# Keeping the split halves of two output weights in DRAM for the second token half

## The chip, the cores and the metric

The kernel runs on one core of one Trainium2 chip. The metric is the device time of one execution in microseconds, from the first instruction of the program to the last, as the runtime reports it. The profiled execution has a time of its own, and its span (first to last traced instruction) is a little shorter than that time.

## The reference

One decoder layer over 1024 tokens of 1024 channels, all in float32:

```
x = x + 1/2 * SwiGLU_1(RMSNorm(x))
h = RMSNorm(x)
[c_q | k_a | v_a | k_idx | w_idx | q_b | k_b | v_b | g_a | g_b] = h @ W_in
y_a = sparse attention (indexer scores -> top 256 keys of each query)     # (1024, 512)
y_b = stick-breaking attention                                            # (1024, 512)
merged = sigmoid(g_a) * (y_a @ w_o_a) + sigmoid(g_b) * (y_b @ w_o_b)      # (1024, 1024)
x = x + merged @ w_out
x = x + 1/2 * SwiGLU_2(RMSNorm(x))
```

The part at issue is the two products `y_a @ w_o_a` (512 x 1024 weights) and `merged @ w_out` (1024 x 1024 weights). Both are computed for one half of the tokens (512 rows) at a time, so each weight is used twice.

## The kernel before

**Split operands.** [...] Each operand is split into a high part (the value rounded, written by ScalarE, line 299 or 1124) and a low part (the value minus the high part, by GpSimd, line 301 or 1126). `mm3` (lines 312 to 314) then multiplies high by high, high by low and low by high into one PSUM bank. A weight piece is 128 x 1024 float32, 512 KB: its load needs one raw tile, its parts need two operand tiles. Splitting one piece takes one ScalarE copy and one GpSimd subtraction, and this is done again each time the piece is used.

**The weights come in pieces.** `w_o_a` is read in four pieces of 256 output columns (`d` = 0, 2, 4, 6). `w_out` is read in eight pieces, `n` = 0, 1 (column halves) by `j` = 0, 2, 4, 6 (pairs of 128-row blocks).

**The order of the work around the change.**

1. The attention stage is written as generators. A planner (`Weave`) with its own costs resumes whichever is ready first, and so fixes the order of TensorE, VectorE, ScalarE and GpSimd by hand. The weights arrive through `Feed`, which keeps three pieces coming; `weights()` loads a piece through the SP queue into the ring `oraw` (2 tiles) and splits it into the ring `ow` (4 tiles, so two pieces). At its end `project("oa", ...)` multiplies token half 1 by `w_o_a` (tiles named `oa0` to `oa6`, PSUM `psoa`), and `merged` stores the gated result to `md` in DRAM. The last two entries of the feed are the first two pieces of `w_o_a` once more (`woa0`, `woa2`), for the other half.
2. The `M0` loop (lines 2247 to 2263) multiplies the other token half by `w_o_a` (tiles `woa0` to `woa6`, PSUM `psm`). VectorE multiplies by a gate and adds the other branch (lines 2261, 2262, operands loaded at lines 2254, 2255), and the sum is split into eight tiles `M0` (lines 386, 387).
3. `project(0, M0, x0, merged)` multiplies the `M0` half by `w_out` (tiles `wout000` to `wout016`, PSUM `psout`). At `n` = 1, `j` = 2 it calls `merged`, which loads the other half's rows back from `md` (`m10r` to `m16r`, through the same ring of raw tiles) and splits them into `M1`.
4. `project(1, M1, x1, between)` multiplies the `M1` half by `w_out` again (tiles `wout100` to `wout116`); for `n` = 1 it holds all four pieces and finishes one row block after the other. The tiles of the second feed-forward block (`b0r`, `b1r`, `by`, `pst`) begin beside it.

From step 2 on the order on each engine and on the SP queue is made by the framework's scheduler, which simulates a timeline. Its tiles come from two rotations. `raw` has four places, two in the `outer` pool and two in `ring2`. `op` has nine, four in `outer` (tag `w`) and five in `ring2` (tag `r`):

```
op = in_turn((wt, 4), (lambda name: pool.tile([P, 1024], F32R, tag="r", name=name, bufs=NR), NR))
raw = in_turn((rawt, 2), (lambda name: pool.tile([P, 1024], F32, tag="raw", name=name, bufs=2), 2))
```

A tile in a rotation is written only when the work on the one that had its place, transfers from it included, is over. Each queue (SP's for loads and most stores, GpSimd's for `put_low` stores) works in order: a transfer that waits for a place holds those behind it. Some pieces of `w_in` already take the way through DRAM: `split_of` names their parts, and `weights()` loads such a piece as two parts.

Of the kernel before, what the change touches and what calls it, by code (L numbers as in the profile page):

```python
# [10 lines left out]
F32 = mybir.dt.float32  # L11
F32R = mybir.dt.float32r
# [10 lines left out]
PE, DVE, ACT, POOL, SP = "PE", "DVE", "Activation", "Pool", "SP"  # L23

P = 128
# [3 lines left out]
ND = D // P  # L29
# [29 lines left out]
def f32(ap):  # L59
    return ap.bitcast(F32)  # L60
# [34 lines left out]
class Weave:  # L95
# [92 lines left out]
    def give(self, *tiles):  # L188
        for t in tiles:
            self.held[t.tensor.name] -= 1  # L190
# [19 lines left out]
    def spawn(self, gen, rank=1, own=None):  # L210
        s = Stream(gen, rank, own or self.own)
        self.streams.append(s)
        self.step(s)
        return s
# [33 lines left out]
def trunk(ctx, tc, x, positions, g_ffn1, w1_gate, w1_up, w1_down, g_mix, w_in, g_cq, w_uq_a, w_q_idx,  # L248
          g_q_a, g_k_a, w_uv_a, w_o_a, w_o_b, w_out, g_ffn2, w2_gate, w2_up, w2_down, inv_freq, out):
    nc = tc.nc  # L250
    cst = ctx.enter_context(tc.tile_pool(name="cst", bufs=1))
    small = ctx.enter_context(tc.tile_pool(name="small", bufs=4))
    dram = ctx.enter_context(tc.tile_pool(name="dram", bufs=1, space=DRAM))
# [50 lines left out]
    def kview(k, n):  # L304
        return lambda raw: (raw[:, 0:k * n].rearrange("p (k f) -> p k f", k=k), k * n)

    def wcols(w, c0, n, k0, k, nm, **kw):
        return split(w[0, k0 * P:(k0 + k) * P, c0:c0 + n].rearrange("(k p) f -> p k f", p=P), nm, kview(k, n), **kw)
# [513 lines left out]

    columns = {f"wg{g}": C_GA + g * P for g in (*range(ND, 2 * ND), *range(ND))}
    columns.update((f"wqk{base}{pr}", base + pr * P) for pr in range(4) for base in (C_QB, C_KB))
    split_of = {nm: [dram.tile([P, 1024], F32, name=f"{nm}{part}d") for part in "hl"] for nm in columns}
    rows_of = w_in[0].rearrange("(k p) f -> p k f", p=P)


    put_high, put_low = nc.scalar.dma_start, nc.gpsimd.dma_start
# [24 lines left out]
    NR, NC_ = 5, 12  # L854
    ctx1, ctxf = ExitStack(), ExitStack()
    fpsum = ctxf.enter_context(tc.tile_pool(name="psf", bufs=1, space=PSUM))
    with tc.tile_pool(name="ring1", bufs=1) as rpool, tc.tile_pool(name="s1", bufs=1) as spool, tc.tile_pool(name="ps1", bufs=1, space=PSUM) as psum:
        op, raw = ring(rpool)
        bank = banks(psum, fpsum)
        sums, pair = of(spool, "s", 5, 512), of(spool, "pair", 2, 512, F32R)  # L860
        with tc.tile_pool(name="t1", bufs=1, side="right") as tpool, tc.tile_pool(name="c1", bufs=1) as cpool:
# [43 lines left out]
            def rows(t):  # L905
                xs.append(fp(tt if t > 3 else ts)(f"x{t}"))
                nc.sync.dma_start(xs[t], x[0, t * P:(t + 1) * P, :])
# [6 lines left out]
            first = [[load(w, q, f"a{e}r0") for q in range(2)] for e, w in enumerate((w1_gate, w1_up))]  # L914
# [86 lines left out]
        def after(n, p):  # L1001
# [10 lines left out]
            if n == 3 and p in range(5, 9):  # L1012
# [6 lines left out]
                     wt=lambda name: rpool.tile([P, 1024], F32R, tag="r", name=name, bufs=NR)) for j in range(2)]  # L1019
# [44 lines left out]
    with fp as fpool, psm as psum, tc.manual_schedule(  # L1064
            engines={nc.tensor.engine, nc.vector.engine, nc.scalar.engine, nc.gpsimd.engine}):
        weave = Weave(nc)
        give, spawn, mark = weave.give, weave.spawn, weave.mark
# [1118 lines left out]
        def merged(ps, load, row, half, to):  # L2186
# [9 lines left out]
            put_low(to, o)  # L2196
            give(o, *held)

        def project(nm, rows, halves, outs):

            for d in range(0, ND, 2):
                W = feed()
                yield PE, W
                wh, wl = W.parts
                for half in halves:
                    for e in range(2):
                        high, low = rows(half)
                        yield PE, high[0] if nm == "ob" else None, fbank
                        ps, r = fbank("ps" + nm), slice((d + e) * P, (d + e + 1) * P)
                        cols = slice(half * 512, half * 512 + 512)  # L2210
                        row, to = (ND + d + e, obd[r, cols]) if nm == "ob" else (d + e, md[r, :])
                        coming = spawn(gate_load(row, d + e, half, nm == "oa"))
                        for k in range(4):
                            yield PE, f"ya0{k}" if nm == "oa" else high[k]
                            c = slice((2 * k + e) * P, (2 * k + e + 1) * P)
                            mm3(ps, wh[:, c], wl[:, c], high[k], low[k], k == 0, k == 3)
                        outs.append(spawn((merged if nm == "oa" else gated)(ps, coming, row, half, to)))
                if nm == "ob":
                    for e in range(2):
                        mark(f"obd{d + e}", *outs[-4:])  # L2220
                give(*W.parts)
# [15 lines left out]
        first = [feed().parts for n in range(2)]  # L2237
# [6 lines left out]
    with ctxf, tc.tile_pool(name="ring2", bufs=1) as rpool, tc.tile_pool(name="ps6", bufs=1, space=PSUM) as psum:  # L2244
        op, raw = ring(rpool)
        bank = banks(psum, fpsum)
        with tc.tile_pool(name="m0", bufs=1) as mpool:
            M0 = []
            for d in range(0, ND, 2):
                wh, wl = first.pop(0) if first else wcols(w_o_a, d * P, 2 * P, 0, 4, f"woa{d}")  # L2250
                for e in range(2):
                    r = slice((d + e) * P, (d + e + 1) * P)
                    g = ht("gate", F32)
                    nc.sync.dma_start(g[:, 0:512], gd[r, 512:1024])
                    nc.sync.dma_start(g[:, 512:1024], obd[r, 512:1024])
                    ps = bank("psm", "bcda"[(d + e) % 4])
                    for k in range(4):
                        c = slice((2 * k + e) * P, (2 * k + e + 1) * P)
                        mm3(ps, wh[:, c], wl[:, c], Y[1][k][:, HI], Y[1][k][:, LO], k == 0, k == 3)
                    m = g[:, 0:512]  # L2260
                    nc.vector.tensor_mul(m, m, ps)
                    nc.vector.tensor_add(m, m, g[:, 512:1024])
                    M0.append(halve(mpool.tile([P, 1024], F32R, tag="m", name=f"m0{d + e}", bufs=8), m, nc.vector))
            hstack.close()
            ctx2, ctx3 = ExitStack(), ExitStack()
            tpool = ctx2.enter_context(tc.tile_pool(name="t2", bufs=1, side="right"))
            tt, ts = of(tpool, "t", 24, dt=F32R), of(tpool, "ts", 4, dt=F32R)
            fp = lambda place: lambda name: f32(place(name))

            def there(t):  # L2270
                return (t + NT // 2) % NT

            def residual(half):
                xs = []
                for q in range(4):
                    xs.append(fp(tt if half else ts)(f"x2{half}{q}"))
                    t = 4 * half + q
                    nc.sync.dma_start(xs[q], xd[there(t) * P:(there(t) + 1) * P, :])
                return xs

            def project(half, M, xs, between=None):

                for n in range(2):
                    c = slice(n * 512, n * 512 + 512)
                    ps = [bank("psout", "abcd"[q]) for q in range(4)]

                    def part(q, j, W):
                        h, l = slice(q * P, (q + 1) * P), slice(512 + q * P, 512 + (q + 1) * P)
                        for k in (j, j + 1):
                            wh, wl = (w[:, (k - j) * 512:(k - j + 1) * 512] for w in W)  # L2290
                            mm3(ps[q], M[k][:, h], M[k][:, l], wh, wl, k == 0, k == ND - 1)

                    def end(q):
                        nc.vector.tensor_add(xs[q][:, c], xs[q][:, c], ps[q])
                        t = 4 * half + q
                        nc.sync.dma_start(x2d[t * P:(t + 1) * P, c], xs[q][:, c])

                    Ws = {}
                    for j in range(0, ND, 2):
                        Ws[j] = wcols(w_out, n * 512, 512, j, 2, f"wout{half}{n}{j}", rawt=raw, wt=op)  # L2300
                        if n and j == 2 and between and not half:
                            between()
                        if not n or not half:
                            for q in range(4):
                                part(q, j, Ws[j])
                    if not n:
                        for q in range(4):
                            end(q)
                        if between and half:
                            between()  # L2310
                    elif not half:
                        for q in range(4):
                            end(q)
                    else:
                        for q in range(4):
                            for j in range(0, ND, 2):
                                part(q, j, Ws[j])
                            end(q)

            x0 = residual(0)  # L2320
            M1 = []

            def merged():
                for d in range(0, ND, 2):
                    m = raw(f"m1{d}r")
                    nc.sync.dma_start(m.rearrange("p (k f) -> p k f", k=2),
                                      md[d * P:(d + 2) * P, :].rearrange("(k p) f -> p k f", p=P))
                    M1.extend(halve(tt(f"m1{d + q}"), m[:, c], nc.vector) for q, c in enumerate((HI, LO)))

            project(0, M0, x0, merged)  # L2330
# [76 lines left out]
```

## Time and profile before

| | |
|---|---|
| median of 3 runs | 2126.56 us (2125.76 to 2130.45) |
| profiled execution, its own time | 2126.26 us |
| its span | 2124.5 us |
| TensorE busy | 2100.6 us, 99% of the span |
| VectorE, ScalarE, GpSimd busy | 72%, 50%, 43% |
| moved by the DMA engines | 387.79 MB, mean 183 GB/s |
| project("oa"), `psoa` | about 1308 to 1359 us |
| `M0` loop, `psm` | 1361 to 1391 us |
| `w_out`, first half, `psout` | 1391 to 1436 us |
| `w_out`, second half, `psout` | 1436 to 1484 us |

The times of the stages are those of the first and the last matmul into the PSUM tile, in us from the start of the span. In lines of the profile, `out<-in` are the tiles written and read, a duration stands behind the start time, and brackets give the idle time of the engine just before the instruction and what ended it. PE is TensorE, DVE VectorE, ACT ScalarE, POOL GpSimd; SPq and POOLq are their DMA queues. A line of a table by windows has the busy time and the instruction count of PE, PEld (weight loads), DVE, ACT and POOL, then the granted TensorE clock, the mean busy share of the 16 DMA engines, and the GB/s they moved.

### The profile page before, as it was taken

The numbers are of one execution on the slowest core, as the hardware profiler recorded it, in microseconds if no ns is written. First come the engines' busy times: TensorE is split into PE (matmuls) and PEld (weight loads), VectorE is DVE, ScalarE is ACT, GpSimd is POOL, SyncE is SP. The second block draws the span as 40 slices with busy tenths as digits, with TensorE's granted clock in tenths as the row PEclk, the third lists the DMA queues.
The fourth block names the chain that finished last, engine by engine and source line by source line (L and its number), as shares of the span: only waits on it lengthen the run. The fifth ranks groups of instructions, "written<-read, shape, count | busy, mean of one in ns | idle before, by whom it ended". The sixth has DMA issues, their size and how long they took to land.

```text
span 2124.5 us, 29820 instructions
## 1 busy us (share of the span) xinstructions
PE 2100.6 (99%) x10196; PEld 1762.4 (83%) x10196; DVE 1521.6 (72%) x2477; ACT 1063.6 (50%) x1998; POOL 913.5 (43%) x717
## 2 busy tenths in 40 slices
PE   8999999999999999999999999999999999999999
PEld 7888888888889988888887888778888888888887
DVE  7866767678875599788886588754755556488675
ACT  6343343334455356888886577535432322324443
POOL 6654555522345234322123342255665545542233
PEclk9999999999999999999999999999999999999999
DMA  5577877497685253686647755574143333259655
GB/s 150 160 245 219 251 203 237 151 328 249 212 231 167 76 159 105 224 217 165 171 157 231 258 165 169 190 257 151 50 129 100 104 95 129 95 185 330 222 175 188
DMA packets 298104, 387.79 MB, mean 183 GB/s; under 512 B 40144, under 2 KB 186224, under 8 KB 297952
## 3 DMA queue, kind: packets, MB, share of 16 engines
q1 hardware_dynamic: 285088, 343.90, 52.2%
q0 software_dynamic: 12864, 41.99, 5.5%
q8 instruction: 80, 1.31, 0.3%
q14 instruction: 72, 0.59, 0.1%
HBM read 264.67 MB, written 121.15 MB: 182 GB/s over the span
## 4 chain that ended last, share of the span: by engine, by line
PE 88%; issue 4%; DVE 3%; DMA 3%; POOL 1%; ACT 1%; SPq 0%; POOLq 0%; DVEq 0%; ACTq 0%
PE p L774 6%; PE p L775 6%; PE p L773 6%; PE pd L535 4%; PE pd L534 3%; PE pd L536 3%; PE pc L534 3%; PE pa L535 3%; PE pa L534 3%; PE pa L536 3%; PE pc L535 3%; PE pc L536 3%; PE psf L312 3%; PE psf L313 3%; PE psf L314 3%
## 5 line engine op out<-in xcount | busy, mean ns | idle before, releaser
L1374 ACT ACTIVATE junka<-u,cand,sig 128x1024 bf16<-128x1024 f32 (+3 forms) x124 | 134.5, 1085 | 5.0 <-DVE cand L1366 3.6
L1820 DVE TENSOR_TENSOR_SCAN left<-left,hidden 128x640 f32<-128x640 f32 (+3 forms) x64 | 88.9, 1409 | 2.0 <-ACT left L1814 1.8
L897 ACT ACTIVATE swh<-swr 128x512 fp32r<-128x512 f32 x48 | 30.2, 629 | 115.5 <-issue 52.5
L898 DVE TENSOR_TENSOR swr<-swr,swh 128x512 f32<-128x512 f32 x48 | 43.6, 908 | 37.8 <-ACT swh L897 37.6
L677 ACT ACTIVATE b0u<-b0u 128x512 f32<-128x512 f32 x20 | 12.6, 632 | 99.8 <-DVE b0u L557 84.4
L1874 DVE SCALAR_TENSOR_TENSOR pt<-pstT,pt 128x512 fp32r<-128x512 f32 (+1 forms) x96 | 51.4, 547 | 14.4 <-ACT pt L1871 13.8
L1871 ACT ACTIVATE pt<-pstT 128x512 fp32r<-128x512 f32 (+1 forms) x96 | 46.6, 495 | 16.6 <-PE pstT L1946 15.1
L1726 ACT ACTIVATE relu<-psdot 128x512 f32<-128x512 f32 (+1 forms) x80 | 40.7, 522 | 26.5 <-DVE u L1733 17.4
L1235 POOL DMA_DIRECT2D gd<-evg x32 | 18.0, 564 | 80.4 <-ACT evg L1230 59.4
L774 PE MATMUL p<-aT,aS 128*128 128x512 f32 x132 | 51.5, 390 | 1.0 <-DVE aT L387 1.0
L774 PE MATMUL p<-bT,bS 128*128 128x512 f32 x132 | 51.3, 389 | 0.0
L1733 DVE SCALAR_TENSOR_TENSOR u<-relu,WI,u 128x512 f32<-128x512 f32 (+1 forms) x70 | 49.2, 718 | 2.7 <-ACT relu L1726 1.7
L775 PE MATMUL p<-aT,aS 128*128 128x512 f32 x132 | 50.7, 389 | 0.0
L775 PE MATMUL p<-bT,bS 128*128 128x512 f32 x132 | 50.7, 389 | 0.0
L2000 ACT ACTIVATE e<-e,mx 128x768 f32<-128x768 f32 (+7 forms) x54 | 40.9, 759 | 13.3 <-DVE mx L1991 13.1
L773 PE MATMUL p<-bT,bS 128*128 128x512 f32 x132 | 47.0, 389 | 0.0
L1946 PE MATMUL pstT<-ident,left 128*128 128x128 f32 x288 | 45.8, 272 | 0.0
L773 PE MATMUL p<-aT,aS 128*128 128x512 f32 x132 | 44.9, 389 | 0.0
L1814 ACT ACTIVATE left<-psz 128x512 f32<-128x512 f32 (+2 forms) x96 | 43.4, 507 | 1.7 <-PE psz L1839 1.6
L1946 PEld LDWEIGHTS pstT<-ident,left 128*128 128x128 f32 x288 | 35.7, 140 | 8.2
L1370 DVE TENSOR_SCALAR_CACHE_REDUCE junkv<-u,cand 128x512 uint8<-128x512 f32 (+1 forms) x62 | 41.7, 673 | 0.8
L386 ACT ACTIVATE bT<-bt 128x512 fp32r<-128x512 f32 x44 | 26.2, 624 | 30.9 <-PE p L775 26.7
(3065 smaller groups left out, 8135.4 us busy)
## 6 DMA issues: line engine op xcount, KB each, us to landing
aw<-in_w_down_dram SPq DMA_DIRECT2D x33, 512.0 KB, 4.9
bw<-in_w_down_dram SPq DMA_DIRECT2D x33, 512.0 KB, 5.0
swr<-in_w_in_dram SPq DMA_DIRECT2D x48, 256.0 KB, 5.6
a0r<-in_w_gate_dram SPq DMA_DIRECT2D x22, 512.0 KB, 7.5
a1r<-in_w_up_dram SPq DMA_DIRECT2D x22, 512.0 KB, 7.2
b0r<-in_w_gate_dram SPq DMA_DIRECT2D x22, 512.0 KB, 4.1
b1r<-in_w_up_dram SPq DMA_DIRECT2D x22, 512.0 KB, 3.9
x<-in_x_dram SPq DMA_DIRECT2D x16, 512.0 KB, 6.2
```

The costliest lines, as they stand in the source:

```text
L312: nc.tensor.matmul(ps, ah, bh, start=first, stop=False)
L313: nc.tensor.matmul(ps, ah, bl, start=False, stop=False)
L314: nc.tensor.matmul(ps, al, bh, start=False, stop=last)
L534: nc.tensor.matmul(ps, a[:, c], b[k][:, HI], start=start and k == 0, stop=False, skip_group_check=True)
L535: nc.tensor.matmul(ps, a[:, c], b[k][:, LO], start=False, stop=False, skip_group_check=True)
L536: ins = nc.tensor.matmul(ps, a[:, l], b[k][:, HI], start=False, stop=k == 3, skip_group_check=True)
L773: nc.tensor.matmul(ps[q][m], S[:, h], T[:, HI], start=p == 0, stop=False)
L774: nc.tensor.matmul(ps[q][m], S[:, h], T[:, LO], start=False, stop=False)
L775: nc.tensor.matmul(ps[q][m], S[:, l], T[:, HI], start=False, stop=p == last)
L1374: nc.scalar.activation(junks[1][:, 0:(i + 1) * P], score[i], AF.Sign, scale=sig[:, b:b + 1], bias=cand.bitcast(F32)[:, b:b + 1], accum_out ...
L1820: nc.vector.tensor_tensor_scan(back, back, ones, 1.0, op0=ALU.mult, op1=ALU.max)
L1946: nc.tensor.transpose(tp[:, q * P:(q + 1) * P], A[n + q][:, j * P:(j + 1) * P], ident)
```

## The change

At its first use each piece's high and low part is also stored to DRAM through GpSimd's queue, and for the other token half the two parts are loaded through SP's queue in place of the raw piece; ScalarE's copy and GpSimd's subtraction of that second use are gone. For `w_o_a`, the new generator `weights_out` stores the parts of `oa0` to `oa6`; since `woa0` to `woa6` are now keys of `split_of`, `weights()` loads `woa0` and `woa2` as parts into `ow`, and the `M0` loop loads `woa4` and `woa6` as parts into `ring2` (tag `r`), where they were split in `outer` before. For `w_out`, `project(0, ...)` stores the parts of its eight pieces and `project(1, ...)` loads them into the `op` rotation, with no raw tile.

```diff
-    split_of = {nm: [dram.tile([P, 1024], F32, name=f"{nm}{part}d") for part in "hl"] for nm in columns}
+    split_of = {nm: [dram.tile([P, 1024], F32, name=f"{nm}{part}d") for part in "hl"]
+                for nm in (*columns, *(f"woa{d}" for d in range(0, ND, 2)), *(f"wout{n}{j}" for n in range(2) for j in range(0, ND, 2)))}
...
+        def weights_out(nm, *parts):
+            for to, w in zip(split_of[nm], parts):
+                weave.held[w.tensor.name] += 1
+                yield POOL, w
+                put_low(to, f32(w))
+                give(w)
+
         def project(nm, rows, halves, outs):
...
                 wh, wl = W.parts
+                if nm == "oa":
+                    spawn(weights_out(f"woa{d}", *W.parts))
...
-                wh, wl = first.pop(0) if first else wcols(w_o_a, d * P, 2 * P, 0, 4, f"woa{d}")
+                if first:
+                    wh, wl = first.pop(0)
+                else:
+                    wh, wl = (rpool.tile([P, 1024], F32R, tag="r", name=f"woa{d}{part}", bufs=NR) for part in "hl")
+                    for w, part in zip((wh, wl), split_of[f"woa{d}"]):
+                        nc.sync.dma_start(f32(w), part)
...
-                        Ws[j] = wcols(w_out, n * 512, 512, j, 2, f"wout{half}{n}{j}", rawt=raw, wt=op)
+                        kept = split_of[f"wout{n}{j}"]
+                        if half:
+                            Ws[j] = [op(f"wout1{n}{j}{x}") for x in "hl"]
+                            for w, d in zip(Ws[j], kept):
+                                nc.sync.dma_start(f32(w), d)
+                        else:
+                            Ws[j] = wcols(w_out, n * 512, 512, j, 2, f"wout0{n}{j}", rawt=raw, wt=op)
+                            for w, d in zip(Ws[j], kept):
+                                nc.gpsimd.dma_start(d, f32(w))
```

## The prediction

> **What bounds the kernel.** I read the engine shares first, then TensorE's waits in the stages of the change, then the DMA load by 10 us windows.
>
> ```profile
> span 2124.5 us, 29820 instructions
> PE 2100.6 (99%) x10196; PEld 1762.4 (83%) x10196; DVE 1521.6 (72%) x2477; ACT 1063.6 (50%) x1998; POOL 913.5 (43%) x717
> ```
>
> TensorE is busy for all but 23.9 us of the span, and the change removes no matmul. It can win only where TensorE waits in these stages, and lose wherever it makes a new wait. TensorE's waits from 1300 to 1500 us:
>
> ```profile
> PE psL L2037 <- DVE mx L1991: 2.4, 2, 2.2
> PE psm L312 <- DVE yt L1893: 1.4, 1, 1.4
> PE psout L313 <- POOL wout000l L301: 1.3, 1, 1.3
> PE pspT L2125 <- DVE mx L1991: 0.2, 1, 0.2
> ```
>
> That is 5.3 us in all, 0.25% of the span. I take 0.2%, 4.25 us, as what a measurement can tell from no change, so even the whole of it is barely a gain that would be seen. The other side is the DMA load:
>
> ```profile
> 1370.00:1380.00 10.00, 10.00 (x39) 8.03 (x38) 3.26 (x5) 1.70 (x3) 1.18 (x1) 0.85 1.01 359
> 1390.00:1400.00 10.00, 8.72 (x38) 6.87 (x37) 9.96 (x8) 4.85 (x6) 9.07 (x4) 1.00 0.31 105
> 1410.00:1420.00 10.00, 10.00 (x46) 8.28 (x45) 5.00 (x9) 5.05 (x9) 0.00 (x0) 1.00 0.92 331
> 1420.00:1430.00 10.00, 10.00 (x46) 8.29 (x45) 2.38 (x4) 1.83 (x3) 4.80 (x2) 1.00 1.01 380
> 1380.00:1436.50 56.50, 55.16 (x242) 44.75 (x240) 32.40 (x37) 20.91 (x28) 30.35 (x13) 1.00 0.72 258
> ```
>
> The last two numbers of a row are the busy share of the DMA engines and their GB/s. The transfers are already full at 1370 to 1380 and 1410 to 1430 us, where 359 and 380 GB/s is what they carry. The room is in the 1390s, at 105 GB/s.
>
> **The change, part by part.** Twelve pieces are stored as 24 parts of 512 KB (0.524 MB): 12.6 MB written. Twelve raw loads become 24 part loads: 6.3 MB more read. Twelve ScalarE copies and twelve GpSimd subtractions go; 24 GpSimd issues come.
>
> ```profile
> 1399.04 2.84 POOL L301 TENSOR_TENSOR wout006l<-wout006r,wout006h 128x1024 fp32r<-128x1024 f32 x1
> L2196 POOL DMA_DIRECT2D md<-o x8: 542/564/697, 1317.5 to 1362.9; - x8
> qad<-qsa POOLq DMA_DIRECT2D x8, 512.0 KB, 3.1
> L312 PE MATMUL psout<-wout006h,m x8: 389/389/389, 1409.1 to 1413.9; 128*128 128x512 f32 x8
> 1393.42 2.85 POOL L301 TENSOR_TENSOR wout002l<-wout002r,wout002h 128x1024 fp32r<-128x1024 f32 x1
> L313 PE MATMUL psout<-wout002l,m x8: 389/389/389, 1399.1 to 1403.2; 128*128 128x512 f32 x8
> ```
>
> *Store issues on GpSimd's queue.* Each holds it some 0.56 us (the `md` store), so two add 1.1 us per piece, and behind them waits the next piece's subtraction. The worst place is the run of four at the start of `w_out`, one after another on GpSimd today: the fourth, `wout006l`, ends at 1401.9; six store issues ahead of it make that 1405.3, and TensorE starts the piece at 1409.1. Cost 0, covered by 3.8 us; at 0.70 us an issue, the longest of that row, still by 3.0. A 512 KB store lands 3.1 us after its issue (`qad`), and only then is its place free; a place is next written four pieces of TensorE's work later, some 20 us, so that is covered too.
>
> *First piece of `w_out`, a gain.* Today GpSimd splits `woa4` and `woa6`, then `wout000`, whose raw tile has to wait for `woa4`'s place. Both splits go, so `wout000` is loaded and split earlier, and the 1.3 us wait goes: -1.3 us. What is late next is `wout002l`, which was ready at 1396.3 and is used at 1399.1, so nothing follows. Bounds -1.3 and 0.
>
> *`woa0`, `woa2` as parts.* Their load can start only when TensorE has left the places of `oa4` and `oa6`; the raw tile was fetched ahead.
>
> ```profile
> L314 PE MATMUL psoa<-y,oa6l x8: 388/389/393, 1350.0 to 1358.8; 128*128 128x512 f32 x8
> woa2r<-in_w_o_a_dram SPq DMA_DIRECT2D x1, 512.0 KB, 3.3
> 1361.33 0.47 PE L312 MATMUL psm<-y,woa2h 128*128 128x512 f32 x1
> 1363.46 0.39 PE L314 MATMUL psm<-y,woa2l 128*128 128x512 f32 x1
> 1363.69 0.39 PE L312 MATMUL psm<-y,woa2h 128*128 128x512 f32 x1
> 1339.18 2.38 POOL L1126 TENSOR_TENSOR oa6l<-oa6r,oa6h 128x1024 fp32r<-128x1024 f32 x1 [5.83 <-ACT oa6h L1124]
> ```
>
> `oa6` is done at 1359.2. The first part lands 3.3 us later, at 1362.5, the second 1.4 us after it (0.524 MB at 380 GB/s). TensorE now uses them at 1361.3 and 1363.5, as filling between the last attention products. It works in order, so a late part holds the products behind it: 1.2 us if the order stays, nothing if other work goes first, 2.1 us if all nine early matmuls (0.23 us apart) move behind the stretch. I take +1.0. On SP's queue the waiting loads stand ahead of `woa4`, whose new place comes free later than these (below); no cost. The stores of `oa0` to `oa6` go out when GpSimd is idle (it waited 5.8 us before `oa6l`): 0. They may shift the planner's order: no row shows that; I bound it by the largest wait there, 2.2 us either way, and take 0.
>
> *`woa4`, `woa6` as parts.* 2.1 MB fall into the full window 1370 to 1380, in place of 1.05 MB that came earlier.
>
> ```profile
> 1367.94 0.37 SPq L297 DMA_DIRECT2D wout002r<-in_w_out_dram x1
> 1379.91 0.39 PE L312 MATMUL psm<-y,woa4h 128*128 128x512 f32 x1
> 1377.39 1.28 DVE L2261 TENSOR_TENSOR gate<-gate,psm 128x512 f32<-128x512 f32 x2 [6.74 <-PE psm L314]
> 1378.60 3.49 DVE L2262 TENSOR_TENSOR gate<-gate 128x512 f32<-128x512 f32 x2
> L2262 DVE TENSOR_TENSOR gate<-gate x8: 679/690/2887, 1378.6 to 1399.5; 128x512 f32<-128x512 f32 x8
> 1386.03 1.88 DVE L387 TENSOR_TENSOR m<-gate,m 128x512 fp32r<-128x512 f32 x3
> 1391.16 1.07 PE L312 MATMUL psout<-wout000h,m 128*128 128x512 f32 x4
> ```
>
> Their new places are free from about 1368 (when the first load into that pool, `wout002r`, was issued); they are needed 12 us later and take 5.8 us at 359 GB/s. If they go first, the gate loads come up to 5.8 us later; VectorE's first product at 1377.4 waits, and TensorE needs `M0`'s first two tiles, ready by 1387.9, at 1391.2 (3.3 us of room). Against it, the two subtractions that slow VectorE here (3.49 us for two adds whose median is 0.69 us) are gone: 2.1 us back. I take 0; bounds -2 and +2.5 (5.8 less 3.3).
>
> *`w_out`, the crowd of transfers.*
>
> ```profile
> 1405.74 0.42 SPq L2326 DMA_DIRECT2D m10r<-md  x1
> 1415.40 0.37 SPq L297 DMA_DIRECT2D wout014r<-in_w_out_dram x1
> 1420.76 2.41 POOL L301 TENSOR_TENSOR wout014l<-wout014r,wout014h 128x1024 fp32r<-128x1024 f32 x1 [11.84 <-ACT wout014h L299]
> L312 PE MATMUL psout<-wout014h,m x8: 389/389/389, 1425.4 to 1430.2; 128*128 128x512 f32 x8
> wout100r<-in_w_out_dram SPq DMA_DIRECT2D x1, 512.0 KB, 9.1
> 1436.54 0.50 PE L312 MATMUL psout<-wout100h,m 128*128 128x512 f32 x1
> 1417.03 1.41 SPq L2278 DMA_DIRECT2D x<-xd  x3
> 1454.60 0.69 DVE L2294 TENSOR_TENSOR x<-x,psout 128x512 f32<-128x512 f32 x1 [3.52 <-PE psout L314]
> ```
>
> From 1380 to 1436.5, where the second half starts, 14.6 MB are moved (258 GB/s times 56.5 us). After: plus 8.4 MB of stores, less the five raw loads of the second half that land by then (2.6), plus the parts of `wout100` and `wout102` (2.1) and 1.05 MB of gate loads that the `woa` parts push past 1380: 23.5 MB. At 380 GB/s the stretch carries 21.5 MB; 2.0 MB, 5.3 us, do not fit. At 358 GB/s (the last window row, 258 at a share of 0.72) it is 3.3 MB, 9 us. Part can be late at no cost: the stores of `wout014` and `wout016` (2.1 MB), the four residual loads from 1417 on, added in at 1454.6 (2.1), and `wout102`, a piece later (1.05): 5.2 MB. But the queues work in order. Two deadlines are near: `wout014l` ends at 1423.2 and is used at 1425.6, with 2.4 us of room, while two pieces' stores (2.1 MB, 5.5 us) come into the stretch from 1405.7 to 1415.4 in which its raw tile waits for the `md` rows to come and go. `wout100` had 9.1 us landings with one transfer and now has two. Bounds 0 (all that is late is what can be) and +9; I take +2.5, nearer the lower end, since the early stores fit into the empty 1390s. In the second half ScalarE and GpSimd lose eight pieces' work, but TensorE has no wait there to win back.
>
> [...]
>
> **Sum.** -1.3 + 1.0 + 0 + 2.5 = +2.2 us on the profiled execution's 2126.26 us (span and 1.8 us around it), which is 0.3 us under the median shown: 2128.5 us.
>
> **The rivals.**
>
> *Slower: the transfers become the bound.* The misfit shows in full as a wait of TensorE for `wout014` or `wout100`: 5.3 to 9 us, 7.2 in the middle, less 1.3: 2132.2 us. It decides from 1.3 + 4.25 = 5.6 us of misfit on. For it: the 380 GB/s row and the 9.1 us landing; against it: 5.2 MB that can wait, and the row with 105 GB/s.
>
> *Faster: the waits go.* With twelve subtractions less, the waits of 2.2, 1.4 and 1.3 us and the slow clock of 1370 to 1380 (0.85, some 1.5 us) vanish: -6.4 us, 2119.9 us; it needs two thirds of it to count. For the 2.2 us wait speaks this:
>
> ```profile
> 1339.20 2.90 DVE L2087 TENSOR_TENSOR y<-yt,y 128x512 fp32r<-128x512 f32 x1
> 1342.75 0.45 PE L2037 MATMUL psL<-kkh,qs 128*128 128x384 f32 x1 [2.21 <-DVE mx L1991]
> ```
>
> An add of 0.69 us takes 2.9 beside the subtraction of `oa6l` (1339.18 to 1341.56, its row stands above), and TensorE waits. But `oa6l` is a first use and stays; only its moment could shift. The 1.4 us hang on the end of attention, which the change leaves alone.
>
> *Nothing at all:* only the 1.3 us go, or not even these, since the transfers find their room: 2125 to 2126.3 us. It lies inside the band of no change.
>
> **How the numbers follow.** Small net change, within 4.25 us either way (the forecast, and nothing at all with it): 0.52, with a range of its own of 2123 to 2130.5. Transfers as the bound: 0.40. Waits gone: 0.08. The likeliest gives 2128.5 us. The range leaves out the far ends: down to 2122.5 (the `w_out` gain and the bound of the planner's shift), up to 2136 (the 9 us end and the +1.0).
>
> **What would show it.** Right: no `wout000l` wait; TensorE waiting in the first half of `w_out` or at its end, by some 1 to 3 us, for a transfer or for `wout014`; a DMA share near 1 from 1400 to 1440. Wrong: more than 5 us of waits for `wout014` or `wout100` (the crowd mis-sized), a wait of TensorE for `woa4` or for `M0` (the gate loads pushed back), or a changed sum of waits before 1360 us (the planner's order).

## The result: slower, by 11 to 17 us

The changed kernel takes 2144.65 us (median of 4, 2143.78 to 2145.33) beside 2127.17 us of the kernel before (2125.76 to 2130.45): a ratio of 1.0080 [1.0062, 1.0097]. Measured again beside later experiments it took 2141.10 us (2140.49 to 2141.46), 1.0054 [1.0039, 1.0069]. Forecast were 2128.5 us and at most 2136. (The interval in brackets is the 95% interval of the ratio of medians.) The profiled execution of the first measurement spans 18.7 us more than before; TensorE's busy time grows by 6.1 us of it, with the same matmuls:

```profile
span 2143.2 us, 29848 instructions
PE 2106.7 (98%) x10196; PEld 1766.1 (82%) x10196; DVE 1517.0 (71%) x2477; ACT 1051.3 (49%) x1986; POOL 893.9 (42%) x729
```

The rest is waiting. TensorE's waits in this execution between 1300 and 1500 us (total, times, longest):

```profile
PE psg L414 <- DMA bg<-in_g_ffn_dram: 5.9, 1, 5.9
PE psout L312 <- ACT wout014h L299: 4.6, 1, 4.6
PE psL L2038 <- DVE mx L1992: 2.4, 2, 2.2
PE psm L312 <- DVE yt L1894: 1.4, 1, 1.4
PE psout L312 <- DMA wout100h<-wout00hd: 0.8, 1, 0.8
PE psout L313 <- POOL wout014l L301: 0.6, 1, 0.6
PE psm L312 <- DMA woa2h<-woa2hd: 0.6, 1, 0.6
```

The 1.3 us for `wout000l` are gone. New are 5.2 us at `wout014` (the piece in the middle of the first token half's second column block), 6.7 us at the start of the second half (the 4 KB of FFN gains, `bg`, whose transpose stands ahead of `wout100`, then `wout100h`), and 0.6 us for `woa2h`. The same execution by windows (TensorE busy first; PEclk, DMA share and GB/s last):

```profile
1410.00:1420.00 10.00, 10.00 (x45) 8.26 (x45) 4.84 (x5) 1.15 (x2) 4.72 (x6) 1.00 1.00 366
1420.00:1430.00 10.00, 6.52 (x29) 5.07 (x27) 2.91 (x6) 2.05 (x4) 0.00 (x0) 1.00 1.04 411
1430.00:1440.00 10.00, 8.29 (x23) 6.07 (x24) 3.32 (x4) 3.29 (x5) 6.84 (x6) 0.66 1.00 341
1440.00:1450.00 10.00, 6.02 (x27) 4.66 (x25) 3.78 (x7) 3.94 (x7) 0.57 (x1) 0.92 1.04 381
1450.00:1460.00 10.00, 7.25 (x26) 6.21 (x27) 3.00 (x10) 0.32 (x2) 1.67 (x3) 0.56 1.06 387
1460.00:1470.00 10.00, 10.00 (x48) 8.28 (x47) 0.01 (x1) 0.73 (x2) 0.00 (x0) 1.00 0.95 358
1380.00:1436.50 56.50, 51.31 (x217) 41.49 (x216) 36.13 (x36) 17.39 (x24) 25.11 (x22) 0.95 0.95 349
1380.00:1470.00 90.00, 78.07 (x326) 63.41 (x325) 42.91 (x54) 22.39 (x34) 29.93 (x28) 0.91 0.98 357
```

From 1410 us on the DMA engines are full, with a share of 0.95 to 1.06 in every 10 us. In the kernel before the long row reads

```profile
1380.00:1470.00 90.00, 88.62 (x404) 72.76 (x403) 50.60 (x64) 41.39 (x59) 47.37 (x23) 1.00 0.66 229
```

that is 20.6 MB in 90 us with a third of the time free, against 32.1 MB after. (The two rows cover the same clock time, not the same work: the changed kernel is behind by then.) Behind the two long waits TensorE's clock falls (0.66, then 0.92 and 0.56), and busy time times the missing share of the clock gives 2.8 + 0.5 + 3.2 = 6.5 us lost on top of 12.5 us of new waits.

**A cleaner measure than the span.** What lies ahead of the change scatters: the first product of the attention output (`psoa`, tile view) starts between 1308.1 and 1313.6 us in all profiles here, whatever was changed. So I also give the stage from there to the last product with `wout116h`: 1308.1 to 1483.8, 175.7 us before; 1310.7 to 1502.7, 192.0 us after. That is +16.3; in the second profile of the same kernel +14.4.

```profile
L312 PE MATMUL psoa<-y,oa0h x8: 389/391/474, 1310.7 to 1318.9; 128*128 128x512 f32 x8
```

```profile
L314 PE MATMUL psout<-wout116h,m x8: 389/389/389, 1490.7 to 1502.7; 128*128 128x512 f32 x8
```

(Tile views of the changed kernel; the numbers after the colon are the shortest, median and longest in ns, then the first and last start.)

### The profile page after: what moved, and what is told of

Its sections match the earlier page's. It is cut to its first block, busy times and chain, and to the rows that moved or that the text cites. A ratio compares the mean times of both kernels' runs of the same rounds, so it can differ in the third digit from the quotient of the medians.

```text
span 2143.2 us, 29848 instructions
## 1 busy us (share of the span) xinstructions
PE 2106.7 (98%) x10196; PEld 1766.1 (82%) x10196; DVE 1517.0 (71%) x2477; ACT 1051.3 (49%) x1986; POOL 893.9 (42%) x729
## 4 chain that ended last, share of the span: by engine, by line
PE 84%; DMA 5%; issue 4%; DVE 3%; ACT 1%; POOL 1%; SPq 0%; POOLq 0%; DVEq 0%; ACTq 0%
PE p L774 6%; PE p L775 6%; PE p L773 6%; PE pd L536 3%; PE pd L535 3%; PE pd L534 3%; PE pa L536 3%; PE pc L534 3%; PE pa L535 3%; PE pa L534 3%; PE pc L536 3%; PE pc L535 3%; PE psf L312 3%; PE psf L313 3%; PE psf L314 3%
## 5 line engine op out<-in xcount | busy, mean ns | idle before, releaser
L677 ACT ACTIVATE b0u<-b0u 128x512 f32<-128x512 f32 x20 | 12.6, 632 | 99.7 <-DVE b0u L557 84.4
L1872 ACT ACTIVATE pt<-pstT 128x512 fp32r<-128x512 f32 (+1 forms) x96 | 46.5, 494 | 16.6 <-PE pstT L1947 15.1
L1727 ACT ACTIVATE relu<-psdot 128x512 f32<-128x512 f32 (+1 forms) x80 | 40.7, 522 | 26.6 <-DVE u L1734 17.5
```

## The experiments

Four theories. **A**: the transfers are the bound, the `w_out` stores above all. **B**: order on SP's queue: the second half no longer uses raw places, so the second FFN's first loads go out ahead of `bg` and `wout100`. **C**: the `w_o_a` part pushes the gate loads, and all behind them, back. **D**: a part can be loaded only once its operand place is free, while a raw tile could be fetched ahead and split later.

| run | what | ratio to before | stage, us more than before |
|---|---|---|---|
| e1 | `w_o_a` part alone | 0.9988 [0.9978, 0.9997] | -2.0 |
| e11 | only `woa4`, `woa6` | 0.9996 [0.9987, 1.0005] | -1.9 |
| e12 | only `woa0`, `woa2` | 0.9992 [0.9983, 1.0001] | -1.1 |
| e2 | `w_out` part alone | 1.0079 [1.0064, 1.0094] | +18.4 |
| e4 | its stores alone | 1.0070 [1.0055, 1.0085] | +13.1 |
| e6 | stores of half the bytes | 1.0029 [1.0018, 1.0040] | +5.5 |
| e7 | stores of columns 0 to 511 | 1.0012 [1.0002, 1.0021] | +2.5 |
| e8 | stores of columns 512 to 1023 | 1.0036 [1.0024, 1.0048] | +6.2 |
| e5 | part loads alone | 1.0016 [1.0007, 1.0025] | +1.1 |
| e3 | change, gains in a place of their own | 1.0075 [1.0060, 1.0090] | +16.7 |
| e9 | change, FFN loads held | 1.0046 [1.0032, 1.0059] | +9.2 |
| e10 | change, TensorE kept busy | 1.0061 [1.0047, 1.0075] | +9.4 |
| e13 | e4, five stores held | 1.0047 [1.0032, 1.0062] | +11.3 |
| e14 | change, stores and FFN loads held | 1.0049 [1.0032, 1.0066] | +13.6 |
| e15 | change again | 1.0054 [1.0039, 1.0069] | +14.4 |

0.1% is 2.1 us. The two columns can differ by some microseconds for one run. The ratio is that of the medians, while the stage comes from one profiled execution, and that lies at the low end of its kernel's times for e1, e4, e5, e8 and e10 and at the high end for e2, e11, e12 and e14.

**Which half of the change: e1, e2.**

```diff
e1: - Ws[j] = [op(...) ...] and the stores     + Ws[j] = wcols(w_out, ...) in both halves
e2: - spawn(weights_out(f"woa{d}", ...)), part loads of woa   + wcols(w_o_a, ...)
```

> Only the w_o_a half of the change (its parts stored at first use, loaded as parts for the other token half); w_out is split twice as before. Theory A (the w_out stores are too much traffic between 1400 and 1460 us): no stores there, so at most 2 us over the kernel before, 2127 to 2130, and no wait for wout014h over 2 us. Theory B (queue order: FFN loads put ahead of the gains and of wout100 once the second half needs no raw places): the second half keeps its raw places here, so also 2127 to 2130. Theory C (the w_o_a part pushes the gate loads and with them the end of the first product, the releases and wout014 back by some 5 to 7 us): the wait for wout014h stays, 4 to 5 us and a slow clock behind it, 2132 to 2137.

> Only the w_out half of the change; w_o_a is loaded and split as before. Theory A: nearly the whole loss stays, 2139 to 2144, with waits for wout014 or the md rows of 4 us or more. Theory B: the wait for the gains (5.9 us in the changed kernel) and the slow clock behind it stay, and nothing ahead of them: 2133 to 2138. Theory C: wout014 comes in time, and what is left is 2 to 4 us under the changed kernel at least: 2132 to 2140, with the wait for wout014h under 2 us.

e1 is 2.6 us faster than the kernel before and has no wait of TensorE at all between 1380 and 1500 us, so theory C falls: its gate loads too are issued 2 to 3 us later than before (the first at 1370.9 us in place of 1368.9, the last at 1382.3 in place of 1379.5), and no wait follows. e2 has the whole loss. Its waits:

```profile
PE psg L414 <- DVE by L434: 4.6, 1, 4.6
PE psout L312 <- ACT wout014h L299: 3.7, 1, 3.7
PE psout L312 <- DMA wout100h<-wout00hd: 1.4, 1, 1.4
```

**The stores alone: e4.** (Half 1 splits `w_out` as before; what is stored is never read.)

```diff
+ if not half: nc.gpsimd.dma_start(d, f32(w))   # per part
  Ws[j] = wcols(w_out, ...)                     # both halves
```

> The kernel before with the 16 stores of w_out's parts added (8.4 MB out on the POOL queue) and nothing else: the second token half still loads and splits w_out itself, and what was stored is never read. Theory A: the stores alone make the crowd, 2135 to 2142, with waits of 3 us or more for wout014, wout016 or the md rows. Theory B: the second half keeps its raw places, so the FFN loads are not put ahead: 2127 to 2131. Theory C: w_o_a is as before, so 2127 to 2131.

14.9 us: the stores alone make most of the loss, as A says, though no FFN load is put ahead here and no part is waited for. The rows of `md` show how (landing time last), and the two largest rows of TensorE's waits:

```profile
m10r<-md SPq DMA_DIRECT2D x1, 512.0 KB, 14.1
...
m14r<-md SPq DMA_DIRECT2D x1, 512.0 KB, 17.3
```

```profile
PE pst L448 <- DVE by L434: 4.2, 2, 3.2
PE psout L312 <- ACT wout014h L299: 2.8, 1, 2.8
```

`m10r` landed in 7.5 us before. `wout014`'s raw tile takes the place of an `md` row that must land and be split first. The row is 6.6 us late, `wout014l` had 2.4 us of room, and TensorE waits 4.0 us for the piece, 2.8 for the high part and 1.2 more for the low. The larger row, for `by`, comes by another way. Two raw tiles of the second half land late (`wout102r` in 15.1 us, 9.7 before), so GpSimd's subtractions of `wout102` and `wout104` run from 1451.6 to 1456.4 us, beside VectorE's scaling of `by`: the first of a pair of these scalings takes 2.56 us there. In the kernel before a pair took 0.88 us with no subtraction of GpSimd beside it (two of the four), and 3.07 and 3.04 us beside one (`wout106l` and `wout112l`). No run tests this second way alone.

Stores issued after `m10r` seem to have slowed it as well: in e8 below one store was issued ahead of the row (at 1403.5 us, the row at 1404.9) and three behind it by 1410.3, and it still took 14.1 us. How the DMA engines divide their time between the two queues, no run shows.

In the whole change the late row is another one, and a second cause stands ahead of it. Counted from the first `psoa` product, `m12r` is issued 6.2 us later than before, and it lands in 12.9 us in place of 8.4, while `m10r` lands in 7.0. First the kernel before, then the changed one:

```profile
1403.12 0.69 DVE L387 TENSOR_TENSOR m<-gate,m 128x512 fp32r<-128x512 f32 x1 [0.70 <-ACT m L386]
1406.20 0.47 SPq L2326 DMA_DIRECT2D m12r<-md  x1
```

```profile
1403.85 7.07 DVE L387 TENSOR_TENSOR m<-gate,m 128x512 fp32r<-128x512 f32 x1 [0.70 <-ACT m L386]
1410.99 3.23 SPq L2293 DMA_DIRECT2D x<-xd  x4
1415.00 0.76 SPq L2349 DMA_DIRECT2D m12r<-md  x1
```

VectorE's last subtraction for `M0` takes 7.07 us in place of 0.69. It runs beside an unbroken run of subtractions and store issues on GpSimd, from 1397.2 to 1414.7 us. The four residual loads (`x<-xd`) stand on SP's queue until that subtraction is over, the queue's own waits say (7.9 us), and `m12r` stands behind them; ScalarE splits `m12r` and `m14r` ahead of `wout014h`. No run takes this cause away alone, and the runs that share it do not lose alike. e15 has it in full (7.08 us, landing 12.9) and waits 5.0 us for `wout014`. e14 below has 8.56 us there and issues `m12r` as late, but there the row lands in 7.7 us, and TensorE waits 1.1 us for the subtraction itself and only 0.5 us for `wout014`. So the late issue by itself brought little; with a slow landing it brought the 5 us.

**Bytes or issues, and which stores: e6, e7, e8.**

```diff
e6: - nc.gpsimd.dma_start(d, f32(w))   + nc.gpsimd.dma_start(d[:, HI], f32(w)[:, HI])
e7: - if not half:   + if not half and not n:          e8: + if not half and n:
```

> As the run with the stores alone, but each of the 16 stores writes only the left half of its part (128x512), 4.2 MB in place of 8.4; the same number of DMA issues in the same places. Theory A by bytes: 4.2 MB is under the 5 MB that could be put off, so most of the 15 us goes, 2128 to 2134. If the number of issues, their 0.55 us each on POOL's queue, or the operand places that the stores hold are the cause, little changes: 2138 to 2144.

> As the run with the stores alone, but only the 8 stores of the first four pieces (columns 0 to 511, 4.2 MB), which go out between 1393 and 1412 us. Theory A: they land on the rows of md asked for at 1404 to 1410 (14 us to land with all the stores, 7.5 us before), so the wait for wout014h stays at 1 to 3 us and the rest goes: 2129 to 2136.

> As the run with the stores alone, but only the 8 stores of the last four pieces (columns 512 to 1023, 4.2 MB), half of them between 1405 and 1413 us, half after 1430. Theory A: 2 MB less stand ahead of the rows of md than with all the stores, wout014 comes in time or less than 1 us late: 2127 to 2133, less than with the first four pieces.

Half the bytes with all 16 issues cost 6.2 us of 14.9 (2133.95 us, at the upper end of what the bytes had been given). Whatever the issues cost by themselves is within these 6.2 us, VectorE's long subtraction included (5.84 us here, 5.88 in e4), and the other half of the bytes makes 8.7 us, so the cost goes with the bytes in the main. The two halves alone cost 2.5 and 7.6 us; together 14.9, not 10.1: room used once is used. I had the order of the two wrong. The later stores cost more: they are issued from 1403.5 us on, just when the `md` rows are asked for, whose slowest landing is 15.1 us in e8 and 12.6 in e7; TensorE waits 3.5 us for `wout014` in e8 and 1.3 in e7, and only in e8 does the clock fall behind it (0.76). The 0.9 us for `wout010h` that e2, e4 and e6 show, and 1.0 in e7, are a place that a store held: in e4 the store landed at 1404.08 and ScalarE's copy began at 1404.12.

**The loads alone: e5.** (It loads kept parts of `w_in`'s gate columns in place of `w_out`'s.)

```diff
- kept = split_of[f"wout{n}{j}"]   + kept = split_of[f"wg{4 * n + j // 2}"]
- nc.gpsimd.dma_start(d, f32(w))
```

> The kernel before with the second half's loads of the change and without its stores: the second token half loads 16 parts of the same size and shape, but those kept of w_in's gate columns (stored long before) in place of w_out's, so its result is another; no w_out part is stored. Theory A (the bytes of the stores are the cause): 2126 to 2129, no wait over 1 us between 1400 and 1470 us. Theory D (a part can only be loaded once its operand place is free, which is when wout016 is used up, where a raw tile could be loaded ahead and split later): a wait of 4 to 7 us for wout100 and 2 to 4 us of slow clock behind it, 2132 to 2138.

```profile
PE psout L312 <- DMA wout100h<-wg0hd: 2.7, 1, 2.7
```

Theory D exists, but it is worth 1.1 us by the stage and 3.4 [1.5, 5.3] by the times, not 5 to 10; the clock stayed at 1.00 behind this wait.

**The gains in a place of their own: e3.**

```diff
- Right(g_ffn2, bank, fp(op), ...)   + Right(g_ffn2, bank, lambda name: cst.tile([P, P], F32, name=name), ...)
```

> The changed kernel with one thing altered: the FFN gains (4 KB) have a place of their own instead of one in the ring of operand places, so their load can go at the start and no load of wout100 stands behind it. Theory B: the 5.9 us wait and most of the slow clock behind it go, 2134 to 2138 (7 to 10 us less than the changed kernel). Theory A: the transfers are the bound, so the wait turns into one for wout100 or wout102 and 0 to 3 us are saved, 2141 to 2145. Theory C says of this wait what A says.

```profile
PE psout L312 <- issue: 7.6, 1, 7.6
PE psout L312 <- ACT wout014h L299: 5.4, 1, 5.4
```

("issue" is a wait for nothing that the profile records.) Nothing was won: `wout100h` now stood where `bg` had stood. SP's queue in the changed kernel and in e3 (start, us):

```profile
1433.97 5.21 SPq L2293 DMA_DIRECT2D x<-xd  x4
1439.28 0.71 SPq L500 DMA_DIRECT2D b0r<-in_w_gate_dram  x1
1440.10 6.72 SPq L410 DMA_DIRECT2D bg<-in_g_ffn_dram  x1
1446.99 0.34 SPq L2319 DMA_DIRECT2D wout100h<-wout00hd  x1
```

```profile
1437.78 0.65 SPq L500 DMA_DIRECT2D b0r<-in_w_gate_dram  x1
1438.61 6.88 SPq L2319 DMA_DIRECT2D wout100h<-wout00hd  x1
```

It is not the gains that are slow, but whatever follows the FFN loads on the queue.

**The FFN loads held, and TensorE kept busy: e9, e10.**

```diff
e9:  + if half and not n and j == 4: load the 4 tiles of w2_gate, w2_up here, in program order
e10: + if n and j == 4 and not half: 30 transposes of ident   # ahead of wout014
     - R.gain()   + R.gain(40)                                # 40 ahead of bg's
```

> The changed kernel with one order altered: the first four loads of the second FFN's weights (2.1 MB), which go out ahead of the gains and of wout100 at 1431 to 1449 us, are held until the second half's loads of wout100 to wout104 have been issued. Theory B (queue order): the gains and wout100h are issued at about 1440 in place of 1446.8, the wait of 5.9 us and the slow clock behind it go, 2134 to 2138. Theory A (bytes): the stores stand ahead of wout014 as before, so the wait of 4.6 us stays, and 0 to 4 us are saved, 2141 to 2145. Theory D (a part's load waits for its operand place): the gains are issued at 1440, but wout100 still waits for places and then 6 us for its landing: 2138 to 2142.

> The changed kernel with TensorE kept busy in its two long waits: 30 transposes of the identity (some 3.5 to 4 us) right ahead of wout014's first product, and 40 (some 5 us) ahead of the gains' transpose; their results are not used, and all transfers stay as they are. If the slow clock behind each wait is a loss of its own: PEclk stays at 1.00 between 1430 and 1460 us and 5 to 8 us are saved, 2136 to 2140. If what follows would have to wait for the transfers in any case: the clock is full, waits for wout016 or wout102 take the place, 2141 to 2145.

In e9 `bg` goes out in 0.55 us, and the wait at the start of the second half falls from 6.7 to 2.5 us; the one at `wout014` stays:

```profile
PE psout L312 <- ACT wout014h L299: 5.4, 1, 5.4
PE psout L313 <- DMA wout100l<-wout00ld: 2.2, 1, 2.2
...
PE psout L312 <- DMA wout102h<-wout02hd: 0.3, 1, 0.3
```

In e10 the clock is full behind the second wait (1.00 where it was 0.56):

```profile
1450.00:1460.00 10.00, 10.00 (x51) 8.47 (x50) 2.73 (x4) 5.02 (x8) 0.00 (x0) 1.00 1.06 391
```

Both medians came out where B and the clock theory put them (2136.75 and 2138.89 us), but not all of that is theirs. Both profiles also lack the 2.2 us wait for `mx` near 1345 us, ahead of every altered instruction. Less that, their stages are 3.0 and 2.8 us under the changed kernel's second profile. That is one pair of profiles each, and the times do not show it: 1.0046 and 1.0061 stand beside 1.0080 and 1.0054 for the changed kernel, and both intervals overlap that of the second, [1.0039, 1.0069]. In e10 the clock behind the first wait is still 0.85, and TensorE still waits 3.4 us at `wout014` and 1.8 at the start of the second half, so the run also shortened waits and does not weigh the clock alone.

**Bytes, or only their order: e13, e14, e15.**

```diff
+ if f"{n}{j}{x}" in ("06l", "10h", "10l", "12h", "12l"): held.append((d, w))
+ while n and j == 4 and held: store them, in program order   # behind wout014's split
```

> The run with the stores alone, same 16 stores and bytes, but five of them (wout006l, wout010h, 010l, 012h, 012l, 2.6 MB) are issued only after wout014's subtraction, behind wout014's own two stores. If the stores cost by sharing the engines with the md rows: these land in 8 to 10 us in place of 14, wout014 comes in time or under 1.5 us late, and over half of the 13 to 15 us goes, 2130 to 2135. If the bytes as such are too many between 1400 and 1460 us: the wait moves to wout016 or to the second half's pieces and under a third goes, 2138 to 2143.

> The whole change with both orders mended: the same five stores held until wout014 is split, and the second FFN's first four loads held until wout100 to wout104 have been issued. By sharing and order: no wait over 2 us at wout014 and at wout100, 2127 to 2133. By bytes: waits of 4 us or more at wout016, wout100 or wout102, 2134 to 2140.

> The changed kernel itself, beside the two above. If the slow clock near 1345 us (a 2.2 us wait for DVE's mx in the attention stage, then 3.7 us lost) differs from one execution to the next, its times spread by some 4 us and its profile may lack it: 2139 to 2146. If it belongs to the kernel: 2143 to 2146 with the wait there again.

e13 does what it should at the place: no wait for `wout014` is left, and `m10r` lands in 9.9 us. But much of the loss moves on (its largest rows in `w_out`; the one for `wout000l` is the old wait):

```profile
PE psout L312 <- ACT wout100h L299: 2.3, 1, 2.3
PE psout L313 <- POOL wout000l L301: 1.3, 1, 1.3
PE psout L313 <- POOL wout100l L301: 1.2, 1, 1.2
PE psout L312 <- ACT braw L469: 1.2, 1, 1.2
```

```profile
wout102r<-in_w_out_dram SPq DMA_DIRECT2D x1, 512.0 KB, 18.7
...
wout106r<-in_w_out_dram SPq DMA_DIRECT2D x1, 512.0 KB, 17.8
```

The second half's raw loads now take 18 us. It costs 10.0 us where e4 cost 14.9 (1.8 less by the stage), so a third of the loss goes, at the border of what the bytes had been given. e14, the whole change with both orders mended, is as slow as e15 beside it (1.0049 and 1.0054): `wout014` is down to 0.5 us, and the sum sits at the start of the second half:

```profile
PE psout L312 <- DMA wout100h<-wout00hd: 9.3, 1, 9.3
```

This alone does not make it the bytes, for a store that is held also holds the place of the part it stores, and the second half needs these places. In e14 `bg` was issued at 1439.4 us, just after a held store had landed (1439.25), and so were `wout100l`, `wout104h` and `wout104l`, each within 0.03 us of such a landing; the held stores took 10.5 to 15.9 us to land. In e13 ScalarE's copy into `wout100h` waited for a store that landed at 1442.3, though its raw tile was there at 1438.1. The engines were full at this point (share 1.03 to 1.12 from 1430 to 1470 us in e14), so these two runs leave open how much is the full engines and how much the places. That the bytes make the loss in the main rests on e4 beside e6. What e13 and e14 show is that to hold stores back wins a few microseconds at most.

e15 also tells the scatter. The wait for `mx` is there again, but with the clock at 1.00, where the first profile had 0.83 (first row the changed kernel, second row e15):

```profile
1340.00:1350.00 10.00, 7.79 (x29) 5.76 (x28) 9.73 (x21) 6.64 (x12) 2.95 (x2) 0.83 0.55 171
```

```profile
1340.00:1350.00 10.00, 7.81 (x45) 6.49 (x44) 9.83 (x20) 6.71 (x13) 3.69 (x5) 1.00 0.48 132
```

That is 1.3 us; with the 2.5 us by which e15's stage starts earlier it makes 3.8 of the 4.5 us between the two profiled spans of one kernel.

**The version to keep** is e1, the `w_o_a` part alone: 0.9988 [0.9978, 0.9997], 2.6 us under the kernel before, which is less than the 4.25 us that the prediction took as visible.

## Why the prediction was wrong

*Failed: the term "`w_out`, the crowd of transfers", +2.5 with bounds 0 and +9.* It measured +16.8 us (e2); apart, the stores cost 14.9 (e4) and the loads 3.4 (e5). The step that failed was the reckoning that all but 2 to 3 MB of the added transfers fit in or can wait at no cost. The mechanism was named rightly, and so were both deadlines that broke, `wout014` and `wout100`; what "would show it wrong" was more than 5 us there, and it was 11.9 with the wait for `bg`. Four things were wrong with the size:

- The window ended at 1436.5, where the second half begins, and 5.2 MB were called able to wait. What waits falls on the next 34 us, which the change fills as well, with 8.4 MB of parts in place of 4.2 MB of raw tiles and with FFN loads pulled forward. Over 1380 to 1470 us the row of before has a share of 0.66, so 31 us of room; the 11.5 MB more that were moved need 32 us at 357 GB/s. Put off in the sum, these bytes had no free room behind the window, only what the other transfers left.
- The stretch was taken to be full all along. The rate was not the fault: 380 GB/s came from the best 10 us, but once the engines were full, 60 us carried 364 to 374 GB/s in the changed kernel and 378 in e15. But over the 56.5 us the changed kernel carried 349, 19.7 MB of the 23.5 wanted, and the 3.8 MB left are 10.9 us. The early stores were to fill the empty 1390s, and they did not: 1390 to 1400 us carried 297 GB/s at a share of 0.77, and 204 at 0.59 in e15.
- "Able to wait" was read as "will wait". The packets of both queues took the time of the same 16 engines (in e4, from 1395 to 1450 us, 62.2% of it went to SP's queue and 37.7% to GpSimd's), and the `md` rows that `wout014` hangs on came later: `m10r` landed in 14.1 us for 7.5 in e4, and `m12r` in 12.9 for 8.4 in the changed kernel, where it was issued 6.2 us later besides.
- The slow clock behind a new wait was not counted: 6.5 us by the windows of the first profile. e10's profile gives some 3 us of it back; its times show nothing clear of noise.

The kernel's new waits and clock losses add up: 12.5 + 6.5, and 1.3 us of slow clock near 1345, less the 1.3 us for `wout000l` and the 1.5 us of slow clock near 1370 that the kernel before had, make 17.5 us; the stage is 16.3 longer.

*Only half right.* Store issues on GpSimd, 0: no piece of the first column block is late in the changed kernel, as reckoned. But the reckoning looked at GpSimd alone. VectorE's subtraction of 7.07 us beside that queue, and SP's queue behind it, were not in it. Nor does the cover for the places hold everywhere: without the `w_o_a` part TensorE waits 0.9 to 1.0 us for `wout010h`, whose place a store held (e2, e4, e6, e7).

*Right or nearly so.* First piece, -1.3: its wait is gone in e1, e11 and after. `woa4`, `woa6`, 0 (-2 to +2.5): e11 measured -0.9 [-2.8, +1.1], with the first piece's gain in it. `woa0`, `woa2`, +1.0 (0 to 2.1): e12 measured -1.7 [-3.6, +0.2], so the sign is not shown; the late part shows as predicted (0.3 to 0.6 us for `woa2h`), and whether more than that is won elsewhere was not traced. All of `w_o_a`: -0.3 forecast, -2.6 [-4.7, -0.6] measured. The gate loads did come later, by 2 to 3 us in e1 and so within the 3.3 us of room that the prediction gave them; no wait followed.

*The rivals.* "The transfers become the bound" is what happened, at 2132.2 us for 0.40; its price took over the same window and the same bytes that can wait, and so the same fault. "The waits go" did not come: in e1 only the 1.3 us wait went. "Nothing at all" is out by the measured interval.

## What to carry to other kernels

Before trading an engine's work for DMA bytes, add up the bytes over the whole stretch in which the transfers run full, to where they are idle again. Price them at the full rate, and count as room only the gaps that the order of the queues lets them use; a transfer "that can wait" is worth only the room behind it, and a store that waits keeps its place (here 0.9 to 1.0 us of waiting for `wout010h`). Where the added traffic shares the engines with a load that something hangs on, that load can slow at once (here `m10r`, landing in 14.1 us for 7.5 in e4), so late deadlines break before the total does. And a new wait on TensorE can cost more than its length: in the first profile here 6.5 us of slow clock stood behind 12.5 us of new waits.

## What the hardware did that I had not expected

**The clock.** Behind waits of 4 to 6 us matmuls came every 0.43 us in place of 0.23 for 6 to 7 us (in the first profile of the changed kernel from 1431.1 to 1438.0 us). But 2.2 us of waiting was enough once and not the next time (the two rows above): of the 15 profiles with that wait, 8 show a slow clock behind it (the longest product with `oa4` takes 628 to 632 ns) and 7 do not (476 or 477). The 2.7 us in e5 were not enough (1.00 from 1430 to 1450 us). So the length of a wait alone does not decide it; what else does, no run shows.

**SP's queue stood still.** `bg` held it for 6.72 us. The landing of `wout016r`, which the program makes it wait for, had released ScalarE's `wout016h` at 1434.5. The profile puts the end of the hold down to TensorE (6.0 us, `psout`), but in e9 the same load to the same place went out at 1427.8, ahead of `wout016`'s first product at 1435.4. That nothing in the program held it is thus argued, not shown. `wout100h` in the same place held it for 6.88, and in e9 the FFN loads themselves took 5 us a pair:

```profile
1439.72 5.16 SPq L2328 DMA_DIRECT2D b0r<-in_w_gate_dram  x2
1444.94 5.40 SPq L2328 DMA_DIRECT2D b1r<-in_w_up_dram  x2
```

These loads have rows of 512 B, eight times as many as a part of the same size (in the kernel before, 1032 packets of 512 B to 2 KB were counted from 1395 to 1450 us, with one such load among the transfers). Whether the rows make the hold, no run here settles. In the kernel before, too, one pair of FFN loads held the queue for 4.89 us.
